# Projection and conditioning weights laid out in contiguous blocks on the host, and a planner list with other durations and due times

## The chip, the cores and the metric

The kernel runs on one NeuronCore of one Trainium2 chip. The metric is the device time of one execution in microseconds. "Faster" means less of it. The engines are named as the profile names them: PE is TensorE, PEld its weight loads, DVE VectorE, ACT ScalarE, POOL GpSimd, SP SyncE, whose queue issues most DMAs.

## What is computed

The reference is a two-layer backbone over 512 latent tokens and 256 context tokens with model width 1024, in float32. Layer 0 mixes by a bidirectional gated DeltaNet, layer 1 by grouped-query attention with an axial rotary embedding. The change touches layer 0's first part and the conditioning of both layers:

```python
for i in range(DEPTH):
    shift, scale, gate = jnp.split(sc_lat @ ada_w[i] + ada_b[i], 3, axis=-1)
    shift_c, scale_c, gate_c = jnp.split(sc_ctx @ ada_w[i] + ada_b[i], 3, axis=-1)
    u_lat = rms_norm(h_lat, norm_g[i]) * (1.0 + scale[:, None]) + shift[:, None]
    ...
    y_lat, y_ctx = deltanet_mixer(u_lat, u_ctx, ...) if i % 2 == 0 else attention_mixer(u_lat, u_ctx, ...)
    h_lat = h_lat + gate[:, None] * y_lat
...
# deltanet_mixer, for latents and context:
p = u @ w_in                              # 1024 -> 4096 (q, k, v) + 2048 (z) + 64 (gates)
qkv = silu(centred_dwconv(p[..., :DN_CONV_DIM], conv_w))
...
# chunks of 64 tokens, both directions, 16 value heads over 8 key heads:
a = where(strict, einsum(kb, kc) * decay, 0)
t_inv = triangular_solve(eye + a, eye)    # the inverses
qk = einsum(qc, kc) * decay               # the masked query products
# then a scan over the chunks with t_inv, qk and the state
```

`ada_w` has 2 x 1024 x 3072 values (12.6 MB a layer), `dn_w_in` 1024 x 6208 (25.4 MB).

## The kernel before, in words

One function, `backbone`, issues everything. Its first part, up to about 567 us of the span, is written out from a list; the recurrence over the chunks (`products`, `solve`, `update`), the output projection, layer 1 and the final norm follow it and are written out by hand.

**The front.** The SP queue loads six token tiles of 128 x 1024 (`opened`, L233), then in turn the conditioning weights and the first projection weights. `ada_load` (L280) brings one of four quarters `q`, one half `kh` of the input rows: a tile of 128 partitions x 4 rows x 2 (shift, scale) x 256 columns, 1 MB, in two DMAs, one for shift and one for scale. There are 8 such tiles (`aw`, six buffers). `ada_quarter` multiplies them with the conditioning vectors (`ada_product`, L284, four products with 32 output rows each), `ada_rows` copies the result from PSUM, `ada_turned` (L298) turns it to columns by eight small products, and `ada_applied` adds biases and norm gains. In between, PE transposes the tokens (L256), DVE and ACT compute their root mean squares, and `x_spread` (L274) spreads these over the partitions. For each of 8 slices of 128 model columns, `x_scaled`, `x_high` (L320) and `x_low` (L324) then make the normalised tokens in two float32r parts, `uh` and `ul`. As soon as a slice is there, `k_step` (L458) accumulates that slice's products for the block of gates ("ab", 64 columns) and for key head 0.

**The key heads.** Key heads 1 to 7 are projected one after the other (`k_products`, L458): weights loaded (`k_load`, L439), split in two float32r parts (`k_high` on ACT, `k_low` on POOL or DVE), multiplied in three passes, then a convolution of five taps, SiLU, squares, transposes and stores. Among them lie the gate arithmetic and the late conditioning: eight pairs of tiles of 128 x 4 x 512 (`late_load`, L373; `late_product`, L284; `late_rows`, `late_turned`, `gate_spread`).

**The 40 heads.** The remaining heads, 8 q, 16 v and 16 z (gate heads), come in an order given by the string `order`. Head `n`: `w_load` (L870), `w_high` (ACT, L875), `w_low` (DVE or POOL, L878), two products `gemm_part` (L889) of 512 and 256 tokens, each into one of four PSUM banks called `g`. For q and v follow `centre` (ACT, L896), `taps` (DVE, L904), `squash` (ACT, L914) and `silu` (DVE, L923 for v, L929 for q); for z only `squash` (L912) and `silu` (L921). The bank is free when `silu` has read it. z heads thus put little on DVE.

**The side work.** Beside these heads the six pairs of chunks `t` = 0 to 5 go through three steps. *Mask products*: `keys_loaded` and `decay_rows` (SP, L687, L695) load keys and rows of gate sums; `m_gram` (PE) multiplies keys with keys; `decay` (ACT, L701, L703; for t = 0 and 1 `apart` on POOL and `faded` on ACT) turns the rows into decays; `m_masks_v`, `m_masks_s`, `m_prod` (DVE, L675) and `m_turn_v` (DVE, L756) make the matrices to be inverted. *Inverses*: POOL solves two `t` at a time, in a chain of 31 columns of two instructions (L774, L775), and weighs them (L779, for the last pair on DVE); then `j_turn` (DVE, L793), small products on PE (L802, L826) and copies on ACT (L814, L833) assemble and store them. *Query masks*: the same loads with queries, `q_gram` (L843), `q_masks` (DVE, L852), decays (ACT, L701), `q_prod` (POOL, L675) and `q_store` (L858). At the end `first_matrices` (L965 and after) loads what the recurrence needs first; it comes after the last query masks, whose buffers it takes.

**What sets the order.** Every step is a `Piece` with an engine, a noted duration, a due time, the pieces it comes after and the buffers it takes and holds. `written_out` walks a model clock: again and again it takes, of all pieces that are possible, the one with the earliest start, and of equal starts the one with the earliest due time:

```python
key = (max(r, free[x.engine]), x.due)
```

The instructions are written in that order, and each engine keeps its own in that order on the chip. So durations and due times change no instruction, only the order on each engine. `T0` is the time for which the first of the 40 heads is planned, `SLOT` = 8.8 what a head takes; head `n` has its times around `T0 + 8.8 n`, and the side work's due times count from `T0` as well. `T1` = 44 is the start of the key heads, which are spread between `T1` and `T0`. `since` keeps a piece from being taken earlier; for the loads of the mask products it follows from their due time. All of the side work takes its turn behind the pieces of the key heads (`late_pieces`).

## Time and profile before

| | us |
|---|---|
| median of 3 runs | 1188.38 |
| lowest and highest | 1184.67, 1196.13 |
| the profiled execution | 1191.09 |
| its span, first to last instruction | 1189.3 |
| end of the last front product (L458 of key head 0) | 57.0 |
| first product of the 40 heads | 155.86 |
| first product of the recurrence | 567.25 |

The profile describes one execution. Its busy times are the sums of an engine's instruction times; a wait is idle time of an engine ahead of an instruction, put down to what released it. A row of a table of windows gives the stretch, its length, the busy time of each engine with its count of instructions, the TensorE clock that was granted (1.00 is full), the mean busy share of the 16 DMA engines, and the GB/s that they moved. A row of a timeline gives start and length in us, engine, line, operation, output <- inputs, sizes and count; in brackets stands idle time ahead of it with what ended it.

### The profile page before, as it was taken

What the parts mean: (1) busy time and instruction counts of PE and PEld (TensorE: products, weight loads), DVE (VectorE), ACT (ScalarE), POOL (GpSimd) and SP (SyncE); (2) the same over time, 40 slices, a digit from 0 to 9 for tenths busy, and PEclk for the clock granted to TensorE, in tenths of its full rate; (3) what the DMA queues carried; (4) which work ended last, traced back from release to release, by engine and by line L of the source; (5) the groups of instructions that cost most, each with busy time, mean ns of one, the idle gap of its engine ahead of it and who ended that gap; (6) DMA issues with size and microseconds to landing.
All of it is one profiled execution on the core that took longest, in us unless ns stands there. A gap on an engine that the chain in (4) does not pass through costs nothing. (4 is left out here: it accounts for less than half of the span.)

```text
span 1189.3 us, 27735 instructions
## 1 busy us (share of the span) xinstructions
PE 1137.5 (96%) x10767; PEld 929.8 (78%) x10767; DVE 780.9 (66%) x1645; ACT 735.6 (62%) x1938; POOL 600.6 (51%) x478
## 2 busy tenths in 40 slices
PE   5999999989989999999899999899998999999996
PEld 3777788878877888888566666688887889999885
DVE  5596454798775876772588888445557467667646
ACT  4435453698677755693478998785752236666731
POOL 0153011399999999441285586556744144230810
PEclk9899999989989999999899999999999999999998
DMA  9788945885549544878798995475844112101323
GB/s 323 219 276 228 339 142 150 205 235 148 157 128 270 180 129 156 244 247 232 205 250 245 261 282 134 165 224 181 250 142 133 37 54 72 36 19 54 107 71 89
DMA packets 175350, 208.73 MB, mean 176 GB/s; under 512 B 12626, under 2 KB 134643, under 8 KB 174451
## 3 DMA queue, kind: packets, MB, share of 16 engines
q1 hardware_dynamic: 155282, 195.32, 55.7%
q10 hardware_dynamic: 19936, 11.64, 3.3%
q8 instruction: 85, 1.39, 0.5%
q14 instruction: 47, 0.38, 0.1%
HBM read 166.16 MB, written 40.67 MB: 174 GB/s over the span
## 5 line engine op out<-in xcount | busy, mean ns | idle before, releaser
L1628 PE MATMUL po<-woh,y 128*128 128x512 f32 x384 | 130.0, 403 | 0.7 <-ACT y L1604 0.7
L1470 POOL TENSOR_TENSOR S<-S,glb 128x512 f32<-128x512 f32 x80 | 81.8, 1045 | 77.5 <-PE ks L1461 77.5
L1577 POOL TENSOR_TENSOR wol<-wo,woh 128x1024 fp32r<-128x1024 f32 x32 | 77.2, 2415 | 55.9 <-ACT woh L1570 49.5
L775 POOL TENSOR_TENSOR X<-X,tmp 128x62 f32<-128x62 f32 (+15 forms) x93 | 93.9, 1010 | 7.3
L889 PE MATMUL g_z<-uh,wh_z 128*128 128x512 f32 (+1 forms) x256 | 90.0, 351 | 6.3 <-DVE sil_q L929 4.5
L889 PE MATMUL g_v<-uh,wh_v 128*128 128x512 f32 (+1 forms) x256 | 90.1, 352 | 5.8 <-DVE sil_v L923 5.8
L904 DVE SCALAR_TENSOR_TENSOR acc_v<-g_v,cwv,acc_v 128x510 f32<-128x510 f32 (+3 forms) x128 | 78.1, 614 | 25.2 <-ACT acc_v L896 21.6
L774 POOL TENSOR_TENSOR tmp<-L,X 128x62 f32<-128x62 f32 (+15 forms) x93 | 90.1, 969 | 6.8
L889 PE MATMUL g_v<-ul,wh_v 128*128 128x512 f32 (+1 forms) x256 | 87.9, 344 | 0.0
L889 PE MATMUL g_z<-ul,wh_z 128*128 128x512 f32 (+1 forms) x256 | 87.9, 344 | 0.0
L889 PE MATMUL g_v<-uh,wl_v 128*128 128x512 f32 (+1 forms) x256 | 87.9, 343 | 0.0
L889 PE MATMUL g_z<-uh,wl_z 128*128 128x512 f32 (+1 forms) x256 | 87.6, 342 | 0.0
L1628 PEld LDWEIGHTS po<-woh,y 128*128 128x128 f32 x384 | 72.7, 189 | 16.0 <-ACT y L1604 0.9
L1628 PE MATMUL po<-wol,y 128*128 128x512 f32 x192 | 76.1, 396 | 0.9 <-POOL wol L1577 0.9
L889 PEld LDWEIGHTS g_z<-uh,wh_z 128*128 128x128 f32 x256 | 49.5, 193 | 12.9 <-ACT g_q L914 4.6
L889 PEld LDWEIGHTS g_v<-uh,wh_v 128*128 128x128 f32 x256 | 49.9, 195 | 11.6 <-DVE sil_v L923 6.1
L1602 DVE SCALAR_TENSOR_TENSOR pt<-pt,og,z 128x128 f32<-128x128 f32 x96 | 34.4, 358 | 34.4 <-PE pt L1593 31.5
L1461 PE MATMUL ks<-S,ck 128*64 128x256 f32 x352 | 55.1, 392 | 0.4 <-ACT o L1467 0.4
L1535 DVE TENSOR_TENSOR S<-su,S 128x512 f32<-128x512 f32 x80 | 51.5, 686 | 5.9 <-PE su L1521 3.9
L889 PEld LDWEIGHTS g_v<-uh,wl_v 128*128 128x128 f32 x256 | 49.9, 195 | 5.5
L889 PEld LDWEIGHTS g_z<-uh,wl_z 128*128 128x128 f32 x256 | 49.6, 194 | 5.6
L889 PEld LDWEIGHTS g_v<-ul,wh_v 128*128 128x128 f32 x256 | 50.0, 195 | 4.9
(440 smaller groups left out, 3325.4 us busy)
## 6 DMA issues: line engine op xcount, KB each, us to landing
aw<-in_ada_w SPq DMA_DIRECT2D x16, 1024.0 KB, 8.7
wo<-in_dn_w_out SPq DMA_DIRECT2D x32, 512.0 KB, 3.4
cv<-v_d SPq DMA_DIRECT2D x48, 256.0 KB, 7.3
aw<-in_ada_w SPq DMA_DIRECT2D x16, 512.0 KB, 8.3
w_z<-in_dn_w_in SPq DMA_DIRECT2D x16, 512.0 KB, 4.3
w_v<-in_dn_w_in SPq DMA_DIRECT2D x16, 512.0 KB, 4.1
v_d<-vt ACTq DMA_DIRECT2D x16, 384.0 KB, 4.3
cT<-t_d SPq DMA_DIRECT2D x12, 512.0 KB, 7.6
```

Source lines behind the costliest of these rows:

```text
L774: G.tensor_tensor(tv, bcast(L[:, :, j + 1:, j], 3, j + 1), bcast(X[:, :, j, 0:j + 1], 2, n), ALU.mult)
L775: G.tensor_tensor(X[:, :, j + 1:, 0:j + 1], X[:, :, j + 1:, 0:j + 1], tv, ALU.subtract)
L889: T.matmul(ps[:, :m], w[:, k], u[:, k, c0:c0 + m], start=k == 0 and n_ == 0, stop=k == KT - 1 and n_ == 2)
L904: V.scalar_tensor_tensor(acc[:, c0 + lo:c0 + hi], ps[:, lo + j - 2:hi + j - 2], cwv[:, j, ct:ct + 1], acc[:, c0 + lo:c0 + hi], ALU.mult, A ...
L1461: T.matmul(ks[r0:r0 + 64, w], kq[w][:, hh, r0:r0 + 64], St[hh][:, d], start=True, stop=True)
L1470: G.tensor_tensor(St[hh], St[hh], bcast(g_, 3, P), ALU.mult)
L1535: V.tensor_tensor(St[hh], sj, St[hh], ALU.add)
L1577: G.tensor_tensor(wl, raws.pop(n), halves[n][0], ALU.subtract)
L1602: V.scalar_tensor_tensor(pj, pj, og, raw(z, off, [[st_, 2], [1, 64]]), ALU.mult, ALU.mult)
L1628: T.matmul(acc[:, nh], y[i][:, j, :], ww[k][:, nh * 512:(nh + 1) * 512], start=h == 0 and x == 0, stop=h == VH - 1 and x == 2)
```

## The change

The host lays three weights out anew, so that what a DMA brings to one partition lies in one piece: `dn_w_in` in 48 heads of 128 partitions x 8 x 128, the 64 gate columns apart as `dn_w_ab`, the first two thirds of layer 0's `ada_w` in the tiles of `ada_load`, and the rest in the tiles of `late_load`. The loads take these blocks whole. `ada_load` becomes one DMA instead of two. On the chip the tiles, their sizes and all arithmetic stay as they were.

In the list the noted durations of `x_spread`, `ada_quarter`, `ada_turned`, `k_step`, `late_product` and `late_turned` grow, `T0` goes from 135 to 140, two pairs of heads change places in `order`, and the due times of mask products, inverses and query masks become others.

```diff
-    w_in = a["dn_w_in"][0].rearrange("(k p) n -> p k n", p=P)
...
     def ada_load(q, kh):
         awt[q, kh] = st.tile([P, 4, 2, 256], F32, tag="aw", name=f"aw{q}{kh}", bufs=6)
-        src = a["ada_w"][0].rearrange("(p k) (v n) -> p k v n", k=KT, v=3)[:, kh * 4:kh * 4 + 4, 0:2, q * 256:(q + 1) * 256]
-        for v in range(2):
-            dma(awt[q, kh][:, :, v], src[:, :, v])
+        dma(awt[q, kh], a["ada_first"][q, kh])
...
-        dma(w, a["ada_w"][i].rearrange("(p k) n -> p k n", k=KT)[:, kh * 4:kh * 4 + 4, nb * 512:(nb + 1) * 512])
+        dma(w, a["ada_late"][nb + 2 * i - 4 * (1 - i), kh])
...
-        dma(kw[h][:, :, :m], w_in[:, :, c0:c0 + m])
+        dma(kw[h][:, :, :m], a["dn_w_ab"] if h == "ab" else a["dn_w_in"][c0 // P])
...
-    order = "zqzqzqqzqqzqqzvvzvvzvvzvvzvvzvvzvvzvvzzz"
+    order = "zqzqzqqzqqzqzqvvzvvzvvzvvzvvzvvzvvvzvzzz"
...
-        dma(raw_w[n], w_in[:, :, c0:c0 + P])
+        dma(raw_w[n], a["dn_w_in"][column[c] + h])
...
-    T0 = 135
+    T0 = 140
...
-    sp = Piece("PE", 0.9, 0.0, x_spread, ...)
+    sp = Piece("PE", 1.5, 0.0, x_spread, ...)
...
-            pr.append(Piece("PE", 0.6, -60, ada_quarter, q, kh, ...))
+            pr.append(Piece("PE", 1.1, -60, ada_quarter, q, kh, ...))
...
-        rt = Piece("PE", 0.5, -60, ada_turned, q, ...)
+        rt = Piece("PE", 1.0, -60, ada_turned, q, ...)
...
-            steps[h].append(Piece("PE", 1.05, 20 + 3 * k + (h == 0), k_step, h, k, ...))
+            steps[h].append(Piece("PE", 1.2, 20 + 3 * k + (h == 0), k_step, h, k, ...))
...
-        pr = [K("PE", 1.15, e - 20, late_product, i, nb, ...)]
+        pr = [K("PE", 2.1, e - 20, late_product, i, nb, ...)]
...
-            tu = K("PE", 0.95, e - 20, late_turned, nb - 2, ...)
+            tu = K("PE", 1.9, e - 20, late_turned, nb - 2, ...)
...
-    for t, due in enumerate(T0 + x for x in (26, 40, 60, 76, 100, 115)):     # mask products
+    for t, due in enumerate(T0 + x for x in (26, 0, 100, 136, 140, 175)):
...
-        due = T0 + (140, 155, 220, 235, 295, 310)[t]                         # inverses
+        due = T0 + (140, 195, 260, 275, 335, 390)[t]
...
-    for t, due in enumerate(T0 + x for x in (170, 200, 230, 260, 290, 320)): # query masks
+    for t, due in enumerate(T0 + x for x in (170, 195, 230, 260, 340, 365)):
...
+    wi = given["dn_w_in"][0]
+    given["dn_w_in"] = wi[:, :6144].reshape(KT, P, 48, P).transpose(2, 1, 0, 3)
+    given["dn_w_ab"] = wi[:, 6144:].reshape(KT, P, 64).transpose(1, 0, 2)
+    w0, w1 = given.pop("ada_w")
+    given["ada_first"] = w0[:, :2048].reshape(P, 2, 4, 2, 4, 256).transpose(4, 1, 0, 2, 3, 5)
+    late = [x.reshape(P, 2, 4, -1, 512).transpose(3, 1, 0, 2, 4) for x in (w0[:, 2048:], w1)]
+    given["ada_late"] = np.concatenate(late)
+    given = {n: np.ascontiguousarray(v) for n, v in given.items()}
```

## The prediction

> **What bounds the kernel now.** I read the page first, then the table of waits, then windows around each wait. The page says TensorE:

> ```profile
> span 1189.3 us, 27735 instructions
> PE 1137.5 (96%) x10767; PEld 929.8 (78%) x10767; DVE 780.9 (66%) x1645; ACT 735.6 (62%) x1938; POOL 600.6 (51%) x478
> ```

> Only what keeps PE idle, or its granted clock low, can be won. The waits of PE (us in total, times, longest):

> ```profile
> PE xt L256 <- DMA ident<-in_ident: 8.1, 1, 8.1
> PE g_v L889 <- DVE sil_v L923: 5.8, 2, 3.3
> PE pa L284 <- DMA aw<-in_ada_w: 4.6, 2, 3.7
> PE g_z L889 <- DVE sil_q L929: 4.5, 1, 4.5
> ...
> PE g_z L889 <- DVE sil_v L923: 1.8, 1, 1.8
> ...
> PE pc L298 <- ACT rows L293: 0.7, 1, 0.7
> ```

> Two groups lie where the change works. In the front the conditioning products wait for their weights (4.6 us, and 0.7 for rows). In the long stage of projection heads a product waits four times for a PSUM bank that DVE has not emptied: 4.5 + 5.8 + 1.8 = 12.1 us. Each wait is followed by a stretch at half clock (columns: length, then busy time of PE, PEld, DVE, ACT and POOL with counts, granted clock, DMA share, GB/s):

> ```profile
> 26.10:36.40 10.30, 9.11 (x36) 5.05 (x36) 6.33 (x11) 2.88 (x6) 1.54 (x1) 0.50 1.09 348
> 254.40:265.10 10.70, 6.21 (x19) 4.85 (x16) 10.49 (x17) 10.67 (x33) 10.07 (x10) 0.68 0.74 208
> 327.30:336.80 9.50, 6.17 (x17) 4.82 (x16) 7.49 (x10) 9.38 (x28) 8.79 (x10) 0.64 0.21 65
> 370.70:377.70 7.00, 4.49 (x26) 4.48 (x26) 4.51 (x5) 6.91 (x15) 7.00 (x4) 0.76 0.58 181
> 474.20:480.10 5.90, 4.10 (x11) 3.26 (x12) 5.86 (x6) 1.41 (x2) 5.90 (x3) 0.71 0.52 189
> ```

> The first row, the front, is 9.1 us of PE work at half clock: 4.6 us lost. In the others (length minus PE busy) is the wait and (1 - clock) x length the loss by clock; I take 0.4 off the first two losses for the part that falls in the wait. Call the stalls a to d: a 4.5 + 3.0 = 7.5; b 3.3 + 3.0 = 6.3; c 2.5 + 1.7 = 4.2; d 1.8 + 1.7 = 3.5; together 21.5 us. The front holds 5.3 + 4.6 = 9.9 us. Between these places, PE has no gap:

> ```profile
> 57.00:153.00 96.00, 96.00 (x749) 73.32 (x749) 64.64 (x147) 46.57 (x107) 31.26 (x42) 1.00 0.86 275
> 153.00:567.00 414.00, 401.18 (x4414) 349.39 (x4412) 282.24 (x424) 279.77 (x682) 275.86 (x232) 0.98 0.65 189
> ```

> So a microsecond won in the front passes whole through the key heads (96.00 of 96.00 busy), and what is won before 567 us passes to the end, since nothing after it is edited.

> **Part 1: the layouts.** No arithmetic is added or removed; there are 8 DMA issues fewer (the front conditioning load is one of 1 MB, not two of 512 KB). Runs grow from 1 KB to 8 KB (front), 2 KB to 8 KB (late) and 512 B to 4 KB (heads). The key-gate block "ab" still lands in 256-byte runs, since its tile keeps 128 columns of which 64 are written. The queue as it is:

> ```profile
> 20.99 1.54 PE L274 MATMUL rr<-dg,on 128*128 128x512 f32 x4
> 22.50 1.06 PE L284 MATMUL pa<-aw,sc 128*32 128x512 f32 x8
> 27.30 1.94 PE L284 MATMUL pa<-aw,sc 128*32 128x512 f32 x8 [3.73 <-DMA aw<-in_ada_w]
> ```

> What long runs are worth I read from the same queue: 4 to 9 us is mostly the latents in 4 KB rows (first line), 28 to 37 us only conditioning weights in 1 KB runs (second):

> ```profile
> DMA packets 919, 2.00 MB, mean 400 GB/s; under 512 B 264, under 2 KB 456, under 8 KB 919
> ```

> ```profile
> DMA packets 3131, 3.13 MB, mean 347 GB/s; under 512 B 94, under 2 KB 3130, under 8 KB 3130
> ```

> 8 KB runs are not in the front; I take 400 GB/s, bounds 347 (no gain) and a little over 400. Ahead of the product at 27.30 lie four front tiles, 4.19 MB: 12.1 us at 347, 10.5 at 400, 1.6 won; the first key head's 0.52 MB gives 0.2. So that product starts at 25.5, and 1.8 us are won whatever stands before it: the other wait for weights, 4.6 - 3.7 = 0.9, goes too, but PE then reaches this one earlier, and waits 2.8 us instead of 3.7. A wait between stall c's 2.5 us (one half-clock stretch of about 3.4 us) and stall b's 3.3 (two) I charge with one, 1.7 us instead of 4.6: 2.9 won. **Front: -4.7**, bounds 0 and -9.9. What is late next there is DVE's chain of scaled tokens, which ends its first at

> ```profile
> 25.65 3.33 DVE L324 SCALAR_TENSOR_TENSOR ul<-y,au,uh 128x256 fp32r<-128x256 f32 x3 [0.67 <-ACT uh L320]
> ```

> so key products could not begin before about 25.5 in any case.

> [...]

> The other transfers are covered (a gate head's weights, KB each and median us to landing):

> ```profile
> w_z<-in_dn_w_in SPq DMA_DIRECT2D x16, 512.0 KB, 4.3
> ```

> The late conditioning loads lie in 57 to 153 us, where PE has no gap; head weights are issued several microseconds ahead of their cast, and no wait above names them. Priced at 0; if the cover went, 4 us a head.

> **Part 2: the list.** The noted durations grow on PE alone: 8 x 0.5 + 4 x 0.5 + 16 x 0.15 + 0.6 + 8 x 0.95 + 2 x 0.95 = 18.5 us, and the heads' origin T0 from 135 to 140. Only order comes of it. The notes had been too small:

> ```profile
> 66.28 1.93 PE L284 MATMUL pa<-aw,sc 128*32 128x512 f32 x16
> ```

> stood at 1.15, now at 2.1; and the first gate head, planned for 135, ran at

> ```profile
> 155.86 0.50 PE L889 MATMUL g_z<-uh,wh_z 128*128 128x512 f32 x1
> ```

> DVE, ACT, POOL and SP thus keep an order made for heads 21 us earlier, so side work stands too far ahead of the heads' own. That makes stalls; no row prices it alone.

> The due times: masks of tile 1 from 40 to 0; tiles 2 to 5 from 60, 76, 100, 115 to 100, 136, 140, 175; inverses and query masks later too. Stall a is this side work:

> ```profile
> 251.66 1.05 DVE L675 TENSOR_TENSOR md<-df_3m,Gx 128x512 f32<-128x512 f32 x1
> 252.63 2.40 DVE L675 TENSOR_TENSOR mo<-df_3m,Gx 128x512 f32<-128x512 f32 x1
> 254.96 2.02 DVE L904 SCALAR_TENSOR_TENSOR acc_q<-g_q,cwv,acc_q 128x254 f32<-128x254 f32 x4
> ```

> Products of tile 3 stand in front of taps and silu, and the bank waits. With tiles 2 and 3 moved 40 to 60 us on, they are not there: **a goes, -7.5**. How full ACT is, all work and the decays of L701 alone, by hundreds:

> ```profile
> 235.00:335.00 100.00, 92.19 (x887) 80.12 (x886) 82.30 (x116) 85.79 (x250) 90.97 (x88) 0.94 0.61 171
> 335.00:435.00 100.00, 97.49 (x1236) 85.32 (x1235) 69.92 (x97) 72.05 (x174) 94.30 (x84) 0.97 0.63 191
> ```

> ```profile
> 235.00:335.00 100.00, 42.97 (x169) 0.94 0.61 171
> 335.00:435.00 100.00, 21.58 (x85) 0.97 0.63 191
> ```

> The first hundred has room to give and the second to take. Tiles 3, 4 and 5 now meet inverses and query masks around stalls b and c, so I count half of those: **-5.3**. Bounds for b and c: -10.5, or worse than before (third rival). Stall d, where DVE weighs the last inverse, is left: 0. The swapped heads (a query head against a gate head, a value head against a gate head at the tail) issue the same instructions: 0, bounds plus or minus one small stall, 3.5.

> POOL must not end later than PE. Its chain of inverses runs from the first to the second of these rows; the last query masks leave for memory at 528.7 (third), and the recurrence, whose first matrices are loaded behind them, starts at 567.25 (fourth):

> ```profile
> 239.81 1.82 POOL L767 MEMSET X<- 128x2048 f32 x1
> ...
> 471.58 0.32 POOL L775 TENSOR_TENSOR X<-X,tmp 128x62 f32<-128x62 f32 x1
> ```

> ```profile
> 528.70 2.69 SPq L858 DMA_DIRECT2D qk_d<-df_5q  x2
> ```

> ```profile
> 567.25 0.67 PE L1487 MATMUL pr<-cv,cT 64*64 64x128 f32 x16 [0.95 <-DVE sil_z L921]
> ```

> 38 us, less some 10 for the store and the loads, against a gain of 18: I charge 0.

> **Sum.** The profiled execution took 1191.1 us. -4.7 - 7.5 - 5.3 = -17.5, so 1173.6. It lay 2.7 over the median of 1188.4, so 1171 in terms of the median; the rivals' times are given so too.

> **Rivals.**
> 1. All four stalls go: -4.7 - 21.5 gives 1162. For it: each hangs on an order made for earlier heads. Against: ACT's second hundred gets fuller.
> 2. The list only moves the stalls, their sum stays: -4.7 alone, 1184. For it: the side work is the same and the engines' room too.
> 3. Slower: the decays of tiles 3 to 5, each as in the row below, 3 x 8.3 = 25 us, enter the second hundred, and 72.1 + 25 is 97 of 100. In stall a's window, where ACT was busy 10.67 of 10.70, 7.5 of 10.7 us were lost, 70%; over 25 us that is 17.6. With a gone and the front: 17.6 - 7.5 - 4.7 = +5.4, so 1194. It makes the kernel slower from 12.2 us of new stalls, and by over 1% from 24.1.

> ```profile
> L701 ACT ACTIVATE df_3m<-df_3m,gcM 128x64 f32<-128x64 f32 x32 | 8.3, 338 | 0.0
> ```

> 4. The copies do not get faster (runs cut up all the same, or memory the limit at 347 GB/s): front 0, list -12.8, 1175.6. The 400 GB/s of the latents speak against it. [...]

> **Numbers.** Chances: forecast 0.42 (own range 1164 to 1180), rival 1 0.20, rival 2 0.22, rival 3 0.08, rival 4 0.08. About 1%, 11.9 us, is what a measurement tells from no change: under 1176.5 is faster. To that go rival 1, four fifths of the forecast's 0.42 and half of rival 4, with a little of rival 2: 0.60. Slower by over 1% takes most of rival 3's spread: 0.06. The rest 0.34. The range 1154 to 1189 holds the forecast and rivals 1, 2 and 4; beyond it lies most of rival 3, and below a front at its bound with all stalls gone and something more.

> **What would show it.** Right: the product now at 27.30 starts near 25.5, key heads about 5 us earlier, DMA near 400 GB/s up to 35 us; no wait on sil_q near 255; ACT's two hundreds level. Wrong: the front's DMA still near 347; new waits of g_v for sil_v between 320 and 400; PE waiting for the first matrices where the recurrence starts.

## The result, and the profile after

The kernel after takes 1173.33 us in the median of 4 runs (1172.76 to 1174.25), beside 1188.54 us for the kernel before on the same chip (4 runs, 1184.67 to 1196.13): a ratio of 0.9865, with a 95% interval of 0.9816 to 0.9914. A second set of runs of the same kernel (experiment 9) gave 1174.99 us and 0.9895 (0.9867 to 0.9923). The profiled execution took 1172.76 us; its span is 18.3 us shorter than that of before. The medians differ by 15.2 us, since the profiled execution of before lay 2.6 us over its median and that of after 0.6 us under. The head of the page after:

```profile
span 1171.0 us, 27730 instructions
...
PE 1127.3 (96%) x10767; PEld 923.8 (79%) x10767; DVE 784.0 (67%) x1645; ACT 734.9 (63%) x1938; POOL 602.6 (51%) x478
```

**Where the 18.3 us came from** is read at three marks that both kernels have: the end of the last key-gate product of the front, the first product of the 40 heads, and the first product of the recurrence. First the kernel before:

```profile
55.67 0.28 PE L458 MATMUL g_kab<-ul,wh_kab 128*64 128x256 f32 x1
```

Then the kernel after, from three windows of the timeline:

```profile
50.16 0.28 PE L455 MATMUL g_kab<-ul,wh_kab 128*64 128x256 f32 x1
...
152.27 0.47 PE L885 MATMUL g_z<-uh,wh_z 128*128 128x512 f32 x1
...
552.01 0.67 PE L1483 MATMUL pr<-cv,cT 64*64 64x128 f32 x16 [0.93 <-DVE sil_z L917]
```

The front ends 5.5 us earlier. The heads begin 3.6 us earlier (155.86 to 152.27), so 1.9 us of the front's gain are lost in the key heads (which part of the change loses them is read below). The heads last 399.7 us instead of 411.4: 11.7 us. From the recurrence's first product to the end it is 619.0 instead of 622.1: 3.1 us, in a part that is not edited. This can't be put down to the change: nearly all of it lies at one place some 350 us into that part, where TensorE waits 3.3 us for `uL` and then runs 3.4 us at half clock in the profile of before, and waits 1.1 us in that of after; experiment 10, with one pair of heads exchanged, has the 3.3 us again, and a second profile of the kernel after (experiment 9) takes 621.2 us for this part. 3.6 + 11.7 + 3.1 = 18.4, the 18.3 of the spans but for rounding.

The waits of TensorE after (us in total, times, longest):

```profile
PE g_z L885 <- DVE sil_v L919: 4.7, 2, 3.6
PE pr L1483 <- ACT vn L1485: 3.3, 2, 2.7
PE GQ L840 <- ACT Tt L830: 2.7, 1, 2.7
PE pa L281 <- DMA aw<-in_ada_first: 2.2, 1, 2.2
...
PE g_q L885 <- DVE wl_q L874: 0.9, 1, 0.9
PE pg L603 <- DVE g_g L594: 0.9, 1, 0.9
```

The waits for sil_q and of g_v for sil_v are gone. Two of over 1 us are new: query products (GQ) wait for a bank that a copy of an inverse (Tt) still holds, and the recurrence's second group waits for vn, 2.7 us instead of 0.7. Where they fall:

```profile
393.94 0.97 PE L840 MATMUL GQ<-kq_2q 128*64 128x64 f32 x16 [2.75 <-ACT Tt L830]
402.73 0.49 PE L885 MATMUL g_z<-uh,wh_z 128*128 128x512 f32 x1 [3.56 <-DVE sil_v L919]
```

So of the four stalls a to d none is left at its place, and one new place with long waits has come. The stages (length, busy time of PE, PEld, DVE, ACT, POOL, clock, DMA share, GB/s), first the front of before, then the kernel after:

```profile
8.00:57.00 49.00, 43.59 (x248) 28.62 (x249) 29.98 (x65) 22.35 (x38) 4.75 (x2) 0.90 0.86 265
```

```profile
8.00:57.00 49.00, 46.14 (x275) 31.71 (x277) 33.98 (x72) 25.12 (x44) 9.68 (x4) 0.97 0.85 324
57.00:153.00 96.00, 95.13 (x761) 72.06 (x761) 63.24 (x148) 46.40 (x105) 26.26 (x40) 1.00 0.74 258
153.00:567.00 414.00, 401.66 (x4560) 350.16 (x4560) 292.83 (x443) 281.79 (x689) 280.39 (x235) 0.99 0.62 192
390.50:406.00 15.50, 9.20 (x71) 8.19 (x71) 11.05 (x16) 14.93 (x39) 14.48 (x16) 0.89 1.00 332
235.00:335.00 100.00, 100.00 (x1092) 87.77 (x1091) 87.56 (x121) 80.07 (x218) 93.84 (x89) 1.00 0.61 176
335.00:435.00 100.00, 93.37 (x968) 81.64 (x967) 73.93 (x104) 77.01 (x196) 94.37 (x83) 0.98 0.60 189
```

PE gains 2.55 us of work in the front and 7 points of clock. The fourth row is the new stall: 6.3 us idle and 0.11 x 15.5 = 1.7 by clock, 8.0 us where the four stalls cost 21.5. ACT's two hundreds, 85.8 and 72.1 before, are 80.1 and 77.0, because its decays are spread (the same two hundreds, line 698 alone, where before had 42.97 and 21.58):

```profile
235.00:335.00 100.00, 33.40 (x130) 1.00 0.61 176
335.00:435.00 100.00, 28.05 (x110) 0.98 0.60 189
```

In the front, the product that waited 3.73 us at 27.30 now waits 2.15 at 24.50:

```profile
24.50 1.07 PE L281 MATMUL pa<-aw,sc 128*32 128x512 f32 x8 [2.15 <-DMA aw<-in_ada_first]
```

and the queue from 20 to 30 us, first before and then after, shows the difference (packets as the profile counts them):

```profile
DMA packets 3894, 3.37 MB, mean 337 GB/s; under 512 B 99, under 2 KB 3893, under 8 KB 3893
```

```profile
DMA packets 633, 4.17 MB, mean 417 GB/s; under 512 B 71, under 2 KB 71, under 8 KB 180
```

A sixth of the packets carries a quarter more bytes, because most are now 8 KB long.

### The profile page after: what moved, and what is told of

The parts are those of the page before. It is cut to its first block, busy times and chain, and to the rows that moved or that the text cites. A ratio compares the mean times of both kernels' runs of the same rounds, so it can differ in the third digit from the quotient of the medians.

```text
span 1171.0 us, 27730 instructions
## 1 busy us (share of the span) xinstructions
PE 1127.3 (96%) x10767; PEld 923.8 (79%) x10767; DVE 784.0 (67%) x1645; ACT 734.9 (63%) x1938; POOL 602.6 (51%) x478
## 5 line engine op out<-in xcount | busy, mean ns | idle before, releaser
L772 POOL TENSOR_TENSOR X<-X,tmp 128x62 f32<-128x62 f32 (+15 forms) x93 | 98.0, 1053 | 7.3
L771 POOL TENSOR_TENSOR tmp<-L,X 128x62 f32<-128x62 f32 (+15 forms) x93 | 86.6, 931 | 6.8
L473 DVE SCALAR_TENSOR_TENSOR acc_k<-g_k,cwv,acc_k 128x510 f32<-128x510 f32 (+3 forms) x64 | 39.3, 615 | 22.7 <-ACT acc_k L466 21.0
## 6 DMA issues: line engine op xcount, KB each, us to landing
wo<-in_dn_w_out SPq DMA_DIRECT2D x32, 512.0 KB, 3.9
w_z<-in_dn_w_in SPq DMA_DIRECT2D x16, 512.0 KB, 4.1
w_v<-in_dn_w_in SPq DMA_DIRECT2D x16, 512.0 KB, 4.0
cT<-t_d SPq DMA_DIRECT2D x12, 512.0 KB, 8.1
```

What stands on the lines that cost most here:

```text
L473: V.scalar_tensor_tensor(acc[:, c0 + lo:c0 + hi], ps[:, lo + j - 2:hi + j - 2], cwv[:, j, 8 + h:9 + h], acc[:, c0 + lo:c0 + hi], ALU.mult, ...
L771: G.tensor_tensor(tv, bcast(L[:, :, j + 1:, j], 3, j + 1), bcast(X[:, :, j, 0:j + 1], 2, n), ALU.mult)
L772: G.tensor_tensor(X[:, :, j + 1:, 0:j + 1], X[:, :, j + 1:, 0:j + 1], tv, ALU.subtract)
```

## The experiments

The first two experiments stood between two theories. A: layouts and list add up; the layouts win in the front alone, the list in the heads alone. B: the shorter transfers also end stalls of the heads. The times, each beside runs of the kernel before on the same chip; "heads" is the profiled time from the heads' first product to the recurrence's first, "rest" from there to the end of the span. The ratio is worked out from all runs and isn't the quotient of the two medians; it differs from that by up to 0.2%, some 2 us, so differences of that size between the rows say nothing:

| kernel | median us | before us | ratio (95%) | heads | rest |
|---|---|---|---|---|---|
| before | | | | 411.4 | 622.1 |
| after | 1173.33 | 1188.54 | 0.9865 (0.9816-0.9914) | 399.7 | 619.0 |
| 1 layouts alone | 1182.20 | 1187.91 | 0.9946 (0.9927-0.9966) | 410.7 | 618.3 |
| 2 list alone | 1179.47 | 1187.91 | 0.9918 (0.9886-0.9949) | 401.6 | 621.9 |
| 3 after, all old due times | 1183.60 | 1187.91 | 0.9956 (0.9935-0.9976) | 414.0 | 612.9 |
| 4 after, old durations and origin | 1176.89 | 1187.91 | 0.9897 (0.9870-0.9923) | 411.2 | 611.2 |
| 5 after, old due times of masks | 1188.00 | 1188.74 | 0.9998 (0.9974-1.0022) | 417.1 | 617.8 |
| 6 after, old due times of inverses and queries | 1178.34 | 1188.74 | 0.9914 (0.9891-0.9938) | 407.5 | 618.1 |
| 7 after, old order of heads | 1177.63 | 1188.74 | 0.9918 (0.9893-0.9944) | 400.6 | 623.8 |
| 8 front layout alone | 1182.40 | 1188.74 | 0.9965 (0.9939-0.9991) | 409.9 | 619.2 |
| 9 after again | 1174.99 | 1186.86 | 0.9895 (0.9867-0.9923) | 401.0 | 621.2 |
| 10 last value head earlier | 1173.67 | 1186.86 | 0.9891 (0.9862-0.9921) | 399.9 | 621.8 |
| 11 two query products later | 1173.66 | 1186.86 | 0.9890 (0.9866-0.9914) | 402.5 | 617.5 |
| 12 new due times of masks alone | 1187.59 | 1186.95 | 0.9986 (0.9964-1.0009) | 410.9 | 622.0 |

Taking from each trace's heads TensorE's idle time, and half of the time for which it worked at half clock, leaves 388.0 to 390.7 us in all 14 profiles; from the rest it leaves 590.0 to 591.7. So, to within 2 to 3 us, waits and half clock are all that sets the kernels apart.

**1, layouts alone.** The kernel before with the loads and the host's reshaping of the diff, none of its numbers:

```
-            dma(awt[q, kh][:, :, v], src[:, :, v])
+        dma(awt[q, kh], a["ada_first"][q, kh])
...
-        dma(w, a["ada_w"][i].rearrange(...)[:, kh * 4:kh * 4 + 4, nb * 512:(nb + 1) * 512])
+        dma(w, a["ada_late"][nb + 2 * i - 4 * (1 - i), kh])
...
-        dma(raw_w[n], w_in[:, :, c0:c0 + P])
+        dma(raw_w[n], a["dn_w_in"][column[c] + h])
```

> The kernel before with the new weight layouts alone (both conditioning matrices, the key, head and alpha/beta weights), the old noted durations, due times, head order and origin of 135. Theory A, the two parts add: the layouts win only in the front, 4 to 6 us; the first conditioning product starts near 24.5 to 25.5 us instead of 27.3, the single half-clock stretch of 10.2 us there shortens to about 3.4, and the four stalls of the 40 heads near 254, 327, 371 and 474 us stand some 5 us earlier and as long as they were; about 1183 us. Theory B, the shorter transfers also end the stalls of the heads: 1174 to 1177 us, with no wait for sil_q near 250. Theory C, without the new durations the written order does not fit the earlier product and the front wins nothing: 1187 to 1189 us.

5.7 us are won, as theory A has it, and the stalls of the heads are all there, the third longer (4.0 us, it was 2.5) and the last shorter (1.1, it was 1.8, and no half clock behind it; waits of TensorE from 160 to 565 us):

```profile
PE g_v L885 <- DVE sil_v L919: 7.3, 2, 4.0
PE g_z L885 <- DVE sil_q L925: 4.6, 1, 4.6
PE g_z L885 <- DVE sil_v L919: 1.1, 1, 1.1
```

Theory B falls. In one thing the expectation failed: no half clock follows the wait in the front, although it is nearly as long as in the kernel after (2.03 us, 2.15); the last part of this document comes back to that. From the front's mark (48.72 us) to the first of the 40 heads (148.91) it is 100.19 us, exactly as in the kernel before and in experiments 8 and 12: with the old list all of the front's gain reaches the heads.

**2, list alone.** The kernel before with the numbers of the diff and its order of heads, none of its loads:

```
-    T0 = 135
+    T0 = 140
...
-    for t, due in enumerate(T0 + x for x in (26, 40, 60, 76, 100, 115)):
+    for t, due in enumerate(T0 + x for x in (26, 0, 100, 136, 140, 175)):
...
-        due = T0 + (140, 155, 220, 235, 295, 310)[t]
+        due = T0 + (140, 195, 260, 275, 335, 390)[t]
...
-    for t, due in enumerate(T0 + x for x in (170, 200, 230, 260, 290, 320)):
+    for t, due in enumerate(T0 + x for x in (170, 195, 230, 260, 340, 365)):
```

> The kernel before with the new list alone (noted durations, origin 140, due times of mask products, inverses and query products, order of the heads), the old layouts. Theory A: the front stays (first conditioning product at 27.3 us, half clock for 7 to 10 us there), the 40 heads win 10 to 12 us because the stalls near 254, 327, 371 and 474 us go; 1177 to 1179 us. Theory B, the heads gain by the layouts: stalls as before, 1186 to 1190 us. Theory C, the durations already reorder the front: part of the front's gain comes here too, 1173 to 1176 us.

8.4 us are won, 9.8 of them in the heads, and the front's wait is as before:

```profile
27.56 1.93 PE L284 MATMUL pa<-aw,sc 128*32 128x512 f32 x8 [3.74 <-DMA aw<-in_ada_w]
```

From the front's mark to the heads it takes 101.67 us, 1.5 more than with the old list: most of what the kernel after loses in its key heads (102.11 us) comes with the new list, and none of it with the layouts alone. 5.7 + 8.4 = 14.1 of 15.2: the two add, within what the intervals allow.

**8, the front's layout alone.** Which layout wins? The kernel before with the first edit of experiment 1 only:

```
-        for v in range(2):
-            dma(awt[q, kh][:, :, v], src[:, :, v])
+        dma(awt[q, kh], a["ada_first"][q, kh])
```

> The kernel before with one edit: the front's conditioning weights laid out by quarters and loaded in one transfer each of 8 KB runs; all other weights as before. Theory A, the layouts' whole gain is this load: 1182 to 1184.5 us, first conditioning product that waits near 24.5 us, last key-gate product of the front ends 49 to 51 us instead of 56.0. Rival, the heads' 4 KB runs or the late conditioning's 8 KB runs carry part of it: 1185 us or more.

1182.4 us, against 1182.2 with all layouts. The pieces of 4 KB of the heads and of 8 KB of the late conditioning are worth nothing that the times can show: their two ratios are 0.9965 and 0.9946, and the intervals overlap. The trace shows half a microsecond in the front, where the product that waits starts at 25.08 us and not at 24.54; there the first key head's weights still come ahead of it in pieces of 512 B.

**3 and 4, inside the list.** Experiment 3 is the kernel after with the three old tuples of due times (the minus lines of experiment 2 for its plus lines, T0 apart). Experiment 4 is the kernel after with the old durations and origin:

```
-    T0 = 140
+    T0 = 135
...
-    sp = Piece("PE", 1.5, 0.0, x_spread, after=[ro], takes=["tr", "tr"], lands=0.1, slack=0.1)
+    sp = Piece("PE", 0.9, 0.0, x_spread, after=[ro], takes=["tr", "tr"], lands=0.1, slack=0.1)
```

and so for the other five durations of the diff.

> The kernel after with the three old tuples of due times (mask products, inverses, query products) and everything else new. Theory A, the due times are what ends the stalls: PE waits for sil_q some 250 us again, the vector engine's hundred from 235 us goes from 87.6 back to about 92 per cent busy, and 7 to 11 us come back: 1180 to 1184 us. Theory B, the origin and the noted durations end them: 1173 to 1176 us with no wait for sil_q over 1 us.

> The kernel after with the old noted durations and the old origin of 135, the new due times, layouts and order of the heads. Theory A, the due times carry the gain: 1173 to 1177 us, front as in the kernel after (product near 24.5 us, last one near 50.4). Theory B, durations and origin carry it: the heads lose 7 to 11 us again, 1180 to 1184 us. A third reading: the durations carry part of the front, then the last key-gate product of the front ends 1.5 us or more after 50.4 us with the heads as in the kernel after.

By the times, due times are worth 10.3 us and durations with the origin 3.6. By the heads it is otherwise: both kernels lose the whole gain there (414.0 and 411.2, beside 399.7; 411.4 before), and both get 6 to 8 us back behind it. In experiment 3 stall a is back at its place (3.7 us at 252.80, put down to ACT's g_q and not to sil_q). Experiment 4 shows where the time comes back. Its heads stall (waits from 160 to 560 us, first fence), but the recurrence then starts without the wait for vn (a window of 14 us at its start, second fence), where the kernel after idles 3.3 us and runs at half clock (third fence):

```profile
PE pw L823 <- issue: 4.7, 2, 3.9
PE g_z L885 <- DVE sil_v L919: 4.3, 2, 3.9
PE g_v L885 <- DVE sil_v L919: 1.9, 1, 1.9
```

```profile
561.00:575.00 14.00, 11.64 (x203) 8.22 (x201) 8.72 (x29) 5.33 (x12) 2.71 (x3) 1.00 0.86 247
```

```profile
551.50:561.50 10.00, 6.74 (x108) 5.34 (x112) 4.38 (x16) 2.93 (x5) 0.00 (x0) 0.66 1.04 292
```

In the kernel after, 3.3 + 0.34 x 10 = 6.7 us are lost in those 10 us. In the first 40 us of the recurrence TensorE is busy 38.92 and 38.56 us in experiments 3 and 4, at full clock; in the kernel after it is busy 35.48, at 0.91. (Experiment 4 has no half clock near 740 us either, the other 2 us of its rest.) It isn't that earlier heads run into a bound there: the kernel before starts its recurrence 15 us later and has the same 35.48 at 0.91, and experiment 5, the latest of all (570.41), has 34.63. What spares experiments 3 and 4 is not shown.

**5 and 12, the due times of the mask products.** Experiment 5 puts the six old numbers back into the kernel after; experiment 12 puts the six new numbers into the kernel before, and nothing else:

```
-    for t, due in enumerate(T0 + x for x in (26, 40, 60, 76, 100, 115)):
+    for t, due in enumerate(T0 + x for x in (26, 0, 100, 136, 140, 175)):
```

> The kernel after with the old due times of the mask products alone (26, 40, 60, 76, 100, 115), everything else new. Theory A, as the prediction has it: the mask products alone make stall a, so PE waits some 4 us for sil_q or g_q near 250 and half clock follows, the later stalls stay gone: 1179 to 1182 us. Theory B, a stall's place is set by the whole order, not by these products: no such wait near 250, 1172 to 1176 us.

> The kernel before with the new due times of the mask products alone (26, 0, 100, 136, 140, 175 after the origin of 135), all else old: layouts, durations, origin, inverses, query products, order of the heads. Theory A, these six numbers carry the heads' gain by themselves, as the kernel after lost all of it without them: 1176 to 1180 us, no wait of TensorE over 1 us between 235 and 335 us, the front as before (product at 27.3 us). Theory B, they need the later inverses, the new durations and the origin beside them: 1183 us or more, with a wait of several microseconds for a bank somewhere from 250 to 540 us.

Without the new masks the whole gain is lost, more than either theory had: 14.7 us, which is also more than with all three old tuples (10.3), and stall a is back (waits from 160 to 565 us):

```profile
PE g_z L885 <- DVE sil_v L919: 7.6, 3, 4.3
PE g_z L885 <- DVE sil_q L925: 4.6, 1, 4.6
PE g_v L885 <- DVE sil_v L919: 3.4, 2, 2.9
```

With the new masks alone nothing is won. Stall a is gone, and others stand in its place (waits from 235 to 560 us, then windows around three of the four places; the fourth is the wait for wl_q, at 235.85):

```profile
PE g_z L889 <- DVE sil_v L923: 7.0, 2, 5.0
PE g_v L889 <- DVE sil_v L923: 2.7, 1, 2.7
PE g_q L889 <- DVE wl_q L878: 2.0, 1, 2.0
```

```profile
339.00:350.00 11.00, 6.04 (x19) 4.72 (x18) 10.68 (x19) 10.94 (x34) 10.29 (x10) 0.69 0.01 3
387.00:395.00 8.00, 5.27 (x21) 4.25 (x20) 4.25 (x7) 7.51 (x17) 7.45 (x9) 0.79 0.59 185
500.00:507.00 7.00, 4.99 (x22) 4.14 (x21) 3.23 (x7) 6.58 (x17) 2.38 (x1) 0.76 0.63 206
```

In the largest, ACT is busy 10.94 of 11.00, as it was in stall a. The decays of the mask products now run until 325 us and end at 352 (294 before), and the query decays of tile 0 (df_0q), which ran from 295 to 309 before, come after them, at 329 to 348, where they meet the copies of the first inverse (Tt). The centring (acc_v), the first step on the way to sil_v, comes late for it, and DVE stands idle 7.7 us for its taps, up to 336.05 (ACT of the same kernel):

```profile
329.00 1.54 ACT L701 ACTIVATE df_0q<-df_0q,gcV 128x64 f32<-128x64 f32 x6 [2.57 <-DMA df_0q<-gc_d]
330.56 3.44 ACT L814 COPY Tt<-U 32x512 f32<-32x512 f32 x6
...
338.64 0.68 ACT L896 ACTIVATE acc_v<-g_v,cwv 128x512 f32<-128x512 f32 x1
```

The masks are needed, and they are not enough: that much of theory B of experiment 12 holds. Which of the other parts they need at the least wasn't tried.

**6, the due times of inverses and query products** put back into the kernel after:

```
-        due = T0 + (140, 195, 260, 275, 335, 390)[t]
+        due = T0 + (140, 155, 220, 235, 295, 310)[t]
...
-    for t, due in enumerate(T0 + x for x in (170, 195, 230, 260, 340, 365)):
+    for t, due in enumerate(T0 + x for x in (170, 200, 230, 260, 290, 320)):
```

> The kernel after with the old due times of the inverses and of the query products, the new ones of the mask products. Theory A: stall a stays gone; inverses and query products of the old places make stalls near 320 and 355 us again, as in the kernel with all three old tuples (10.3 us over the kernel after); 1177 to 1181 us. Theory B, the mask products carry the whole gain of the due times: 1172 to 1176 us. Theory C, new masks meet old inverses and both stalls and ACT's second hundred (335 to 435 us) get worse than in the kernel before: 1184 us or more.

1178.34 us, 5.0 over the kernel after, and 7.8 us in the heads: theory A in size. The waits lie elsewhere than it said; the tuples as a set put query products ahead of their load:

```profile
PE g_z L885 <- DVE sil_v L919: 7.4, 3, 5.6
PE GQ L840 <- DMA kq_2q<-q_d: 2.9, 2, 2.7
PE g_q L885 <- DVE wl_q L874: 2.5, 1, 2.5
```

**7, the order of heads** put back:

```
-    order = "zqzqzqqzqqzqzqvvzvvzvvzvvzvvzvvzvvvzvzzz"
+    order = "zqzqzqqzqqzqqzvvzvvzvvzvvzvvzvvzvvzvvzzz"
```

> The kernel after with the old order of the heads (a query head and a value head against a gate head swapped back). Theory A, the swaps are worth nothing: 1170.5 to 1176 us, the last gate head's product ends within 2 us of 551.1. Rival: the swap at the tail lets the last gate heads' taps-free work clear the banks, 4 us or more come back: 1177 us or more, with a wait of a gate head for sil_v near 530 to 550 us.

The heads take 400.6 us, as in the two profiles of the kernel after (399.7 and 401.0). The 4.3 us more lie behind them: the recurrence's first loads are issued later (the exchanged rows elX at 554.83, against 549.91), and TensorE waits, by way of vd, for what they bring:

```profile
PE su L1517 <- DVE vd L1493: 6.5, 1, 6.5
```

The equal heads are partly luck: those of experiment 7 idle more (10.7 us; 9.6 and 8.5 in the kernel after) and have no half clock, where the two profiles of the kernel after have one step of it and three. The intervals of 7 and 9 overlap (0.9893-0.9944 and 0.9867-0.9923), so that the swap is worth something is likely and not shown.

**9 to 11, two tries for a better version.** The kernel after again (no edit), and one edit each for 10 and 11:

```
-    order = "zqzqzqqzqqzqzqvvzvvzvvzvvzvvzvvzvvvzvzzz"
+    order = "zqzqzqqzqqzqzqvvzvvzvvzvvzvvzvvzvvvvzzzz"
```

```
-    for t, due in enumerate(T0 + x for x in (170, 195, 230, 260, 340, 365)):
+    for t, due in enumerate(T0 + x for x in (170, 195, 260, 290, 340, 365)):
```

> The kernel after, unchanged, beside the two variants below, so that they can be compared with it in one row of runs. Expected: 1172 to 1175 us. [...]

> The kernel after with one more swap in the order of the heads: the last value head goes ahead of the gate head before it (tail vvvvzzzz instead of vvvzvzzz). In the kernel after the recurrence's first copy waits 3.3 us for the load of the values, which stands behind the store of the last value head; one head earlier, that store and load are done before the recurrence starts. Theory A: the wait of 2.7 us of TensorE at 552 us and the half clock behind it go, 3 to 5 us: 1168 to 1171 us. Rival: four value heads in a row overload the vector engine between 500 and 530 us, a new wait of a head for sil_v of 2 us or more takes its place: 1172 to 1178 us.

> The kernel after with the query products of tiles 2 and 3 due 30 us later (260 and 290 instead of 230 and 260). In the kernel after these meet the copies of an inverse near 391 us, the scores of tile 2 wait 2.7 us for their bank, and a gate head waits 3.6 us for sil_v at 399. Theory A: both waits go, 4 to 8 us: 1165 to 1170 us. Rival: the stalls only move to where the two tiles now fall, 420 to 460 us: 1171 to 1178 us.

Neither tells itself apart from the kernel after. In experiment 10 the last values are stored 3.7 us earlier, 538.67 instead of 542.35, and the wait stays:

```profile
550.66 0.67 PE L1483 MATMUL pr<-cv,cT 64*64 64x128 f32 x16 [1.53 <-DVE sil_z L917]
554.29 1.13 PE L1483 MATMUL pr<-cv,cT 64*64 64x128 f32 x16 [2.96 <-ACT vn L1485]
```

So it is not the last value head's way through memory that holds the start. In both kernels the copy to vn follows the store of a gate head on ACT's queue, and whether store or copy waits, and for which load, stays open. In experiment 11 the decays of query tile 2 still run from 380.5 to 402.7 us (380.8 to 403.5 in the kernel after): 30 us of due time moved an order, not the work, and the stall at 391 to 403 stayed (5.7 and 2.2 us, beside 3.6 and 2.7). No version that beats the kernel after was found.

## Why the prediction was right, and where it was not

The forecast was 1171 us and the measurement 1173.3, faster by 1.35%. The sum is right, some of its terms are not, and that they meet is in part luck: of the spans' 18.3 us, beside a sum of 17.5, 3.1 came behind the heads, from the wait for uL that the change isn't shown to touch, and made up for 1.1 us missing in the front and 1.1 in the heads.

**Front, -4.7: the mechanism was right.** The product came to 24.50, not 25.5. The new rate was taken rightly at 400 GB/s; what the sum had too small was the gain over the old one. From 9 us up to the product the old queue moved 6.2 MB at 338 GB/s, and not 4.7 MB at 347; the new one moved the same 6.2 MB at 400 (windows before, then after; the last number is GB/s):

```profile
9.00:27.30 18.30, 12.99 (x83) 8.28 (x82) 13.94 (x31) 10.43 (x18) 2.01 (x1) 0.97 1.10 338
```

```profile
9.00:24.50 15.50, 12.73 (x83) 8.11 (x81) 12.04 (x29) 10.05 (x18) 1.38 (x1) 1.00 1.04 400
```

Half clock fell from 10.2 us to one stretch of 3.4, as the prediction charged it; that it was one is luck, as the last part shows. That is -5.5 at the front's end, and the medians of experiments 1 and 8 are 5.7 and 6.3 us lower. Rival 4, copies no faster, is out. "Passes whole through the key heads" is right for the layouts (100.19 us before and in experiments 1 and 8) and 1.9 us too good for the whole change: the list alone costs 1.5 there (experiment 2), and in the kernel after 0.9 is a new wait (pg for g_g), which leaves PE 95.13 of 96.00 busy where it had no gap. What the other 1.0 us is stays open.

**Head weights and late conditioning loads at 0: right,** within what the times can show (experiment 8).

**"a goes, -7.5": right as to the place, wrong as a term.** Experiments 5 and 12 show both ways that the old due times of the masks make the wait for sil_q near 250. But taking it away alone gave 0.5 us in the heads and no time that can be measured: the decays met other work 85 us later, and the bank waited there. This is rival 2, the list only moves the stalls, and it holds for this part of the list when it stands alone.

**b and c halved, d left: wrong in every single stall, near in the sum.** All four are gone at their places, as rival 1 had it, and 8.0 us of a new one stand at 391 to 406. Forecast for the heads were -12.8, and -11.7 came (-9.8 with the old layouts). The step that failed is the one that prices stalls one by one by the edit next to them. What the runs put in its place is an order whose parts don't add: with any one of masks, durations and origin, or inverses and queries taken out, the heads last 407.5 to 417.1 us instead of 399.7, and the losses, 17.4 + 11.5 + 7.8, are three times the gain. No run shows what b, c and d would be worth one by one.

**Rival 3, ACT's second hundred full: no.** It came to 77.0 and not to 97; the decays of tiles 3 to 5 begin only 12 to 20 us later (259.2, 272.1 and 297.5, against 245.6, 260.4 and 278.0), because the order shifted less than the due times. Yet experiment 12 has its mechanism (83.42 of ACT's second hundred, and the stall at 340).

**Swapped heads at 0: right for the heads,** and open for the time.

**The recurrence's start at 0: right between the two kernels, for a reason that was not given.** 38 us of slack were counted on POOL's chain. What waits there is another thing: the recurrence's own first loads (behind which store they stand is open, by experiment 10). The kernel before already waited for them (between its first groups, from 548 to 590 us, with half clock from 568.8 and from 575.7), and the kernel after does (6.7 us lost), so the two are alike there and the term comes out at 0. PE waiting where the recurrence starts was one of the prediction's signs of being wrong; it came, but it is no loss of the change. Experiments 3 and 4 lose 14.3 and 11.5 us in the heads and only 10.3 and 3.6 in time, mainly because their recurrences start without that. The row of the kernel before:

```profile
PE pr L1487 <- DMA cv<-v_d: 3.8, 2, 2.5
```

## What to carry to other kernels

An entry of a written order has no price of its own: test a part both by taking it out of the new list and by putting it alone into the old one, since here six numbers were worth 14.7 us by the one and nothing by the other. Where transfers are what the first products wait for, count the bytes that lie in one piece: 8 KB against 1 KB gave 400 GB/s against 338 up to the product that waits, and all that the layouts won, and the same edit under cover gave nothing that the times show. Then look at what the next stage loads before it starts: some 6 us were lost or spared there, whichever the edit was meant for.

## What the runs showed of the hardware

```profile
22.09:25.50 3.41, 1.25 (x13) 0.17 (x9) 3.29 (x4) 2.58 (x4) 2.36 (x1) 1.00 1.01 418
25.50:28.91 3.41, 3.41 (x14) 2.47 (x11) 2.38 (x5) 0.98 (x2) 0.00 (x0) 0.50 1.02 413
```

```profile
22.87:26.28 3.41, 1.74 (x12) 0.62 (x13) 3.38 (x5) 2.69 (x5) 2.36 (x1) 1.00 1.01 411
26.28:29.69 3.41, 3.41 (x27) 2.31 (x25) 3.07 (x8) 0.89 (x2) 0.00 (x0) 1.00 1.02 418
```

So a wait of some 2 us was followed by half clock in one execution and not in another; that the phase of the grid decides which is a reading of these cases. The front shows them best: in the kernel after and experiments 3, 5, 6, 7, 9, 10 and 11 it has the same layouts and the same order of instructions on every engine, and the waits are 1.93 to 2.31 us. Experiments 7, 10 and 11 have no half clock there, the kernel after, 3 and 6 one step, 5 and 9 two, and the last key-gate product starts at 49.5 to 49.7, 49.8 to 50.2, and 51.2 to 51.5 us. In the front the border between the two is less sharp: steps with 1.14 us of idle (experiment 5, 19.98 to 23.39) and 1.47 (experiment 9, 20.54 to 23.95) were followed by half clock, and one with 1.49 (experiment 11, 23.14 to 26.55) was not.

**One core's queue carried 417 GB/s** from 20 to 30 us in the kernel after, with pieces of mostly 8 KB, against 337 in the kernel before with 1 KB.
